# A hybrid decoder layer on one core: gates between heads, loads ahead, operands without a store, sums on VectorE

## The chip, the core and the metric

One core of one Trainium2 chip runs the whole program. Five engines work side by side, each through its own queue in order: TensorE (PE: matrix products, into PSUM), VectorE (DVE), ScalarE (ACT), GpSimd (POOL) and the sync engine (SP), which issues most DMAs; POOL and ACT issue some too. The metric is the time of one execution on the device, in microseconds, as the median of several. A difference of 0.3% is about what can be measured here.

## The reference, cut to what matters

One layer, for a prompt of 1024 tokens and for 8 sample sequences of 4 tokens each (32 columns more), all in float32:

```python
proj = x @ w_in                            # q,k,v | hgrn q,f,i,g | gate_a | gate_b
oa = rms_norm((softmax(q1 k1^T) - lam*softmax(q2 k2^T)) v) * (1 - lam_init)   # 4 heads; sample: paged cache, 1024 old tokens
ob = rms_norm(hgrn2_scan(...)) * silu(g)                                       # 4 heads
merged = sigmoid(ga) * (oa @ w_branch_a) + sigmoid(gg) * (ob @ w_branch_b)
h = layer_norm(ALPHA * x + merged @ w_out)
a, g = split(h @ w_up);  c = conv3(a) + b                                      # D_FF = 2816
out = layer_norm(ALPHA * h + (gelu(c) * g) @ w_down)
```

## The kernel before, in words

**Products.** Every operand of a large product is split into a rounded part and a remainder (`split`, L131: a cast on ScalarE, L132, a subtraction on VectorE, L133), and each product is three matmuls (L238 to L240). So whatever PE reads costs both engines some time first.

**Order.** The program is written in the order below. A planner lays each engine's queue out from it: it runs the program against its own estimate of durations and gives an engine the earliest instruction in program order that it holds ready. On the chip each queue is then fixed. A tile of a tag with n buffers waits until one of these is given back.

**Attention and gates.** The input projection is done in pieces. The sixteen gate blocks (`do_gates`, L845, through `proj_gate`, L830) are 72 matmuls each, a tanh and a store to DRAM (`gsc`). Two run before the first head, three after head 0, two after head 1, and nine after head 3, in the loop at L950. A head (`attn`, L615) goes through eight blocks of queries: scores, maximum, exponential, difference of the two softmaxes, transposes, product with v; its output goes to DRAM (`osc`).

**Sample.** `SampleAttn` works through the cached pages beside other work: sixteen steps (`beside`, L942), eight of keys and then eight of values. A step fetches two pages of 1 MB by indirect DMA from POOL's queue (L726) into two buffers; for keys VectorE transposes them (L746), PE multiplies (L752 for keys, L803 for values). The last value step of each group of four stores its output (`oss`). Before, ten steps stand in the gates' loop, four in the first half's merge (after every second block), two after its tiles 1 and 3.

**Merge, in two halves of the tokens.** `load_o` (L925) loads attention's output, eight tiles `Ot[k]` of 128 rows, splits it into the tags q0 to q7. `merge` (L1018) multiplies it by the branch weights in eight blocks m, with the gates in tags "ae" and "c", into `Mg`; then the output product, tile by tile of 128 tokens (`w_out`, two halves of columns), the LayerNorm statistics (L1106 to L1118), and `turn_` (L1055), which transposes the normalised rows on PE, scales and shifts the eight pieces (two of each four on VectorE, L1070, two on ScalarE, L1072) into "hs" tiles, and stores them to DRAM (`hT`, L1073, POOL's queue). `turn_` of a tile runs one tile late; that of the last tile is put into `pending`, which the next stage runs. The second `load_o` stands after the first merge.

**Operands of the up projection.** It is done as seven products instead of eight, of quarters of the operand (B11, B12, B21, B22) and of their sums (`combine`, L993: four sums, five pairs put; `put`, L983, splits). A quarter pair comes from token tile t of the first half and tile t + 4 of the second (`tile_operands`, L1008). Tiles 4 and 5 are summed straight from `turn_`; tiles 6 and 7 are loaded back from `hT` (`quad`, L987), tile 6's after the merge, tile 7's after the first chunk of the first up block. "hs" has three buffers, "ae" and "c" two.

**Up, conv, down.** Twenty-two up blocks m, each in two chunks of columns (256 and 272); the products are evacuated through two "hs" tiles (`Mt`, `Xt`, L1183), convolved in a row that lives in slots 2 and 3 of `rt` by turns (m even in 2, odd in 3), and stored (`uT`). `down_half` (L1240) loads the 22 tiles in pairs, through one buffer of its own and `rt` 2 and 3 in turn, splits them and multiplies.

Of the kernel before, what the change touches and what calls it, by code (L numbers as in the profile page):

```python
# [44 lines left out]
def hybrid_step(ctx: ExitStack, tc: tile.TileContext, I, O):  # L45
# [835 lines left out]
    do_gates(2)  # L881
    Q, K = proj_q(1, q_slots()), K1
    attn(2, Q[0], K[0], v[0])
    sample_new_scores()
    attn(3, Q[1], K[1], v[1])
    psx.close()
# [35 lines left out]

    wba, wbb, wout = I["w_branch_a"][0], I["w_branch_b"][0], I["w_out"][0]

    def load_o(th, nh):  # L925
        Ot = [qt(k) for k in range(8)]
        for k in range(8):
            raw = wide(("hs", "ae")[k % 2])
            if k < 4 or nh == 512:
                SY.dma_start(raw[:, :nh], osc[k][:, th:th + nh])  # L930
            else:
                SY.dma_start(raw[:, :512], osc[k][:, th:th + 512])
                SY.dma_start(raw[:, 512:nh], oss[k - 4])
            split(raw[:, :nh], Ot[k][:, 0, :nh], Ot[k][:, 1, :nh])
        return Ot

    av = avs.enter_context(tc.tile_pool(name="av", bufs=1))
    ap = aps.enter_context(rpool("ap"))
# [8 lines left out]
        if len(steps) == 8:  # L947
            aps.close()

    for n in (2, 1, 1, 1, 1, 1, 1, 1, 1):  # L950
        do_gates(1)
        if len(gates) == 2:
            Ot = load_o(*HALVES[0][:2])
        beside(n)
    px.close()

# [36 lines left out]
    def combine(c, cols, b11, b12, b21, b22, t3):  # L993

        G.tensor_tensor(t3, b22, b12, ALU.subtract)
        G.tensor_tensor(b12, b12, b11, ALU.subtract)
        put(c, B22, cols, b22)
        G.tensor_tensor(b22, b22, b12, ALU.subtract)
        put(c, T2, cols, b22)
        G.tensor_tensor(b21, b21, b22, ALU.subtract)  # L1000
        put(c, T1, cols, b12)
        put(c, T3, cols, t3)
        put(c, T4, cols, b21)
# [1 line left out]
    def tile_cols(t):  # L1005
        return t // 2, slice(t % 2 * 128, t % 2 * 128 + 128)

    def tile_operands(t, b12=None, b22=None):  # L1008

        c, cols = tile_cols(t)  # L1010
        if b12 is None:
            b12, b22 = quad("ae", 0, 1, t), quad("c", 1, 1, t)
        b11, b21 = quad("ae", 0, 0, t), quad("c", 1, 0, t)
        combine(c, cols, b11, b12, b21, b22, wide("hs")[:, :512].rearrange("p (k t) -> p k t", k=4))

# [2 lines left out]
    def merge(Ot, half, beside=None):  # L1018
# [5 lines left out]
        for m in range(8):  # L1024
# [18 lines left out]
            if beside and m % 2:  # L1043
                beside(1)


        tiles = (4, 5, 8, 6, 7) if half else tiles
        rr = []
# [5 lines left out]

        def turn_(r, t, tt, tn):  # L1055

            ys = f2.tile([128, 2, 4, TS], F32, tag="ys", name="ys") if t == 8 else None
            yy = []
            for h2 in range(2):
                p = (ps_s.tile([128, 512], F32, tag="s", name="ps_s") if h2 else pst()).rearrange("p (k t) -> p k t", k=4)  # L1060
                y = ys[:, h2] if t == 8 else wide("hs")[:, :512].rearrange("p (k t) -> p k t", k=4)
                yy.append(y)
                for k4 in range(4):
                    k = h2 * 4 + k4
                    transpose(p[:, k4, :tn], r[:tn, k * 128:(k + 1) * 128])
                for k4 in range(4):
                    k = h2 * 4 + k4
                    g1, b1 = pt[:, P_L1G + k:P_L1G + k + 1], pt[:, P_L1B + k:P_L1B + k + 1]
                    if k4 >= 2:
                        V.tensor_scalar(y[:, k4, :tn], p[:, k4, :tn], g1, b1, ALU.mult, ALU.add)  # L1070
                    else:
                        S.activation(y[:, k4, :tn], p[:, k4, :tn], AF.Identity, bias=b1, scale=g1)  # L1072
                G.dma_start(hT[h2][half][:, :, tt - th:tt - th + tn].rearrange("k p t -> p k t"), y[:, :, :tn])  # L1073
            if t == 8:
                ts_ = f2.tile([128, 4, 16], F32, tag="ts", name="ts")
                cols = slice(256, 272)
                b = [ys[:, i, :, j:j + 16] for i in range(2) for j in (0, 16)]
                put(1, B11, cols, b[0])
                put(1, B21, cols, b[2])
                combine(1, cols, *b, ts_)  # L1080
            elif t in (4, 5):
                tile_operands(t - 4, *yy)

        if half:
# [8 lines left out]
        for hf, some in ((0, tiles[:2]), (1, tiles), (0, tiles[2:])) if half else ((0, tiles), (1, tiles)):  # L1093
            w = w_B(wout, hf * 512, 512)
            for t, r in zip(tiles, rr):
                if t not in some:
                    continue
                tt, tn = tok(t)
                lt = tt - th
                ps = pmm()  # L1100
                rv = r[:tn, hf * 512:(hf + 1) * 512]
                if t < 8:
                    mm3(ps, [((Mg[k][:, 0, lt:lt + tn], Mg[k][:, 1, lt:lt + tn]), w[k]) for k in range(KD)])
                else:
                    mm_s(ps[:2 * TS], Ms, w)
                    V.scalar_tensor_tensor(rv, rv, 2.0 * ALPHA, ps[TS:2 * TS], ALU.mult, ALU.add)  # L1106
                V.scalar_tensor_tensor(rv, rv, 2.0 * ALPHA if t < 8 else 1.0, ps[:tn], ALU.mult, ALU.add)
                st = sts[:, t % 4 + (t == 8) * 4]
                V.bn_stats(st[:tn, hf], rv)
                if t not in done:  # L1110
                    done.add(t)
                    if beside and t % 2:
                        beside(1)
                    continue
                mu, rs = aggr(st, tn, 4.0 * EPS)
                nm = f2.tile([128, 1], F32, tag="nm", name="nm", bufs=2)[:tn]
                V.tensor_scalar(nm, mu, rs, -1.0, ALU.mult, ALU.mult)
                S.activation(r[:tn], r[:tn], AF.Identity, bias=nm, scale=rs)  # L1118
                for x in late:
                    turn_(*x)  # L1120
                late = [(r, t, tt, tn)]
        pending.extend((lambda x=x: turn_(*x)) for x in late)

    merge(Ot, 0, beside)
    avs.close()
    h0.append(ups.enter_context(tc.tile_pool(name="h0", bufs=1)))
    Ot = load_o(*HALVES[1][:2])
    merge(Ot, 1)
    tile_operands(2)


    w_up, w_dn = I["w_up"][0], I["w_down"][0]
# [39 lines left out]
    for m in range(NM):  # L1172
# [7 lines left out]
        S.copy(aes[:, :, 0:2], st_conv[:, m])  # L1180
        for c, cn in enumerate(CHUNK):
            x = ops[c]
            Mt, Xt = wide("hs"), wide("hs")  # L1183
            m1, m5, u3, u4 = Mt[:, :cn], Mt[:, 272:272 + cn], Xt[:, :cn], Xt[:, 272:272 + cn]
            o = c * 256

# [17 lines left out]
            if m + c == 0:  # L1204

                while pending:
                    pending.pop(0)()
                tile_operands(3)
        for hf, tag in enumerate(("ae", "c")):
            cc, o = wide(tag), hf * 512  # L1210
            S.activation(cc[:, :512], ae[:, o + 2:o + 514], AF.Identity, bias=cb, scale=cw[2])
# [28 lines left out]
    def down_half(half, before=None):  # L1240
# [2 lines left out]
        U = []  # L1243
        for k in range(NM):
            if k % 2 == 0:
                j = k // 2 % 3
                raw = rt(j + 1, (2, 544)) if j else us.tile([128, 2, 544], F32, tag="ur", name="ur")
            SY.dma_start(raw[:, k % 2, :nh], uT[k][:, th:th + nh])
            u = ut(k)
            split(raw[:, k % 2, :nh], u[:, 0, :nh], u[:, 1, :nh])  # L1250
            U.append(u)
# [189 lines left out]
```

## Time and profile before

| | |
|---|---|
| Median of 3 runs | 1845.83 us (1841.52 to 1846.64) |
| Profiled execution, its span | 1842.59 us, 1840.1 us |
| PE, PE's weight loads busy | 1730.7 us (94%), 1618.0 us (88%) |
| VectorE, ScalarE, POOL busy | 1103.8 us (60%), 765.5 us (42%), 579.4 us (31%) |
| Read from HBM, written | 172.44 MB, 40.41 MB |

The profile is one execution. Times of rows are microseconds from the span's start. In the slices, a digit is a share in tenths over a fortieth of the span. In a timeline, a row is one instruction or a run of equal ones; the last bracket is the engine's idle time before it and what ended that. PE's matmuls are pipelined, so a row's time is longer than the step from one to the next.

### The profile page before, as it was taken

How to read it: one execution, taken by the hardware profiler on the slowest of the kernel's cores; microseconds unless marked ns; L12 is line 12 of the kernel's file. 1: busy time of each engine (PE TensorE's matmuls, PEld its weight loads, DVE VectorE, ACT ScalarE, POOL GpSimd, SP SyncE). 2: the span in 40 equal slices, each digit the busy share in tenths (PEclk: the TensorE clock that was granted, in tenths of full speed). 3: DMA queues.
4: the chain of work that ended last, by engine and by line, in shares of the span. 5: the costliest groups of instructions: out<-in, count | busy, mean ns of one | idle time of the engine just before them, and what ended most of it. 6: DMA issues, size and time to landing. Idle time of an engine off the chain costs nothing.

```text
span 1840.1 us, 34341 instructions
## 1 busy us (share of the span) xinstructions
PE 1730.7 (94%) x13412; PEld 1618.0 (88%) x13412; DVE 1103.8 (60%) x2327; ACT 765.5 (42%) x1775; POOL 579.4 (31%) x735
## 2 busy tenths in 40 slices
PE   8999999999999798989979949999999997999995
PEld 8999999999999597967879749999999996888995
DVE  5767546654656655525466857767776776338435
ACT  6466253445553452213243534434444444325222
POOL 1000110430413122213121466776677663001003
PEclk9999999999999999989989869999999998999997
DMA  6110211221211028778576322322222227436443
GB/s 212 35 60 25 81 60 41 90 67 59 85 63 54 1 87 282 245 279 296 196 220 205 101 70 70 98 72 76 79 88 73 76 70 251 124 111 204 133 125 109
DMA packets 215273, 215.07 MB, mean 117 GB/s; under 512 B 11212, under 2 KB 182174, under 8 KB 211016
## 3 DMA queue, kind: packets, MB, share of 16 engines
q1 hardware_dynamic: 190944, 136.04, 24.5%
q0 software_dynamic: 17040, 67.99, 10.3%
q10 hardware_dynamic: 7128, 8.86, 1.4%
q8 instruction: 105, 1.72, 0.4%
q14 instruction: 56, 0.46, 0.1%
HBM read 172.44 MB, written 40.41 MB: 116 GB/s over the span
## 4 chain that ended last, share of the span: by engine, by line
PE 48%; DMA 7%; DVE 4%; issue 3%; ACT 2%; POOL 1%; SPq 0%; ACTq 0%; POOLq 0%; DVEq 0%
PE mm L1268 4%; PE mm L1267 4%; PE mm L1269 4%; PE mm L1168 4%; PE mm L1167 4%; PE mm L1166 4%; PE mm L238 3%; PE mm L239 3%; PE mm L240 3%; PE ps_s L1167 2%; PE ps_s L1168 2%; PE ps_s L1166 2%; PE tp L1167 2%; PE tp L1168 2%; PE tp L1166 2%
## 5 line engine op out<-in xcount | busy, mean ns | idle before, releaser
L133 DVE TENSOR_TENSOR wl<-raw,wh 128x512 fp32r<-128x512 f32 x378 | 271.6, 728 | 235.2 <-ACT wh L132 195.8
L132 ACT CAST wh<-raw 128x512 fp32r<-128x512 f32 x378 | 226.7, 609 | 405.5 <-PE mm L1268 116.7
L238 PE MATMUL mm<-xh,wh 128*128 128x384 f32 (+1 forms) x560 | 186.9, 334 | 0.4 <-ACT wh L132 0.3
L240 PE MATMUL mm<-xh,wl 128*128 128x384 f32 (+1 forms) x560 | 186.4, 333 | 0.0
L239 PE MATMUL mm<-xl,wh 128*128 128x384 f32 (+1 forms) x560 | 185.9, 332 | 0.0
L238 PE MATMUL mm<-wh,xh 128*128 128x256 f32 x480 | 136.0, 284 | 1.4 <-DVE rb L581 1.4
L239 PE MATMUL mm<-wl,xh 128*128 128x256 f32 x480 | 136.3, 285 | 0.2 <-DVE wl L133 0.2
L240 PE MATMUL mm<-wh,xl 128*128 128x256 f32 x480 | 135.7, 284 | 0.0
L1267 PE MATMUL mm<-q,wh 128*128 128x512 f32 (+2 forms) x384 | 124.8, 325 | 0.0
L1269 PE MATMUL mm<-q,wl 128*128 128x288 f32 (+2 forms) x384 | 124.7, 326 | 0.1
L1268 PE MATMUL mm<-q,wh 128*128 128x512 f32 (+2 forms) x384 | 124.4, 324 | 0.0
L240 PEld LDWEIGHTS mm<-xh,wl 128*128 128x128 f32 x560 | 105.4, 188 | 3.7 <-issue 3.6
L238 PEld LDWEIGHTS mm<-xh,wh 128*128 128x128 f32 x560 | 105.3, 188 | 2.6 <-issue 1.5
L239 PEld LDWEIGHTS mm<-xl,wh 128*128 128x128 f32 x560 | 105.5, 188 | 0.9 <-issue 0.6
L238 PEld LDWEIGHTS mm<-wh,xh 128*128 128x128 f32 x480 | 90.3, 188 | 2.0 <-issue 1.6
L239 PEld LDWEIGHTS mm<-wl,xh 128*128 128x128 f32 x480 | 90.2, 188 | 1.0 <-DVE wl L133 0.8
L240 PEld LDWEIGHTS mm<-wh,xl 128*128 128x128 f32 x480 | 90.3, 189 | 0.1
L1276 POOL DMA_DIRECT2D c<-hT x24 | 13.0, 540 | 221.9 <-PE mm L1269 76.2
L1167 PE MATMUL mm<-h,wh 128*128 128x256 f32 x264 | 75.8, 287 | 3.4 <-DVE h L133 3.4
L1166 PE MATMUL mm<-h,wh 128*128 128x256 f32 x264 | 75.6, 286 | 2.5 <-ACT wh L132 2.5
L1267 PEld LDWEIGHTS mm<-q,wh 128*128 128x128 f32 x384 | 72.5, 189 | 5.7
L1269 PEld LDWEIGHTS mm<-q,wl 128*128 128x128 f32 x384 | 72.4, 189 | 5.7 <-DVE wl L133 0.3
(504 smaller groups left out, 5492.1 us busy)
## 6 DMA issues: line engine op xcount, KB each, us to landing
raw<-in_w_in_dram SPq DMA_DIRECT2D x44, 512.0 KB
raw<-in_w_up_dram SPq DMA_DIRECT2D x44, 512.0 KB
raw<-in_w_down_dram SPq DMA_DIRECT2D x36, 512.0 KB
raw<-in_w_out_dram SPq DMA_DIRECT2D x20, 512.0 KB
raw<-in_w_down_dram SPq DMA_DIRECT2D x18, 384.0 KB
gsc<-gt ACTq DMA_DIRECT2D x32, 192.0 KB
uT<-ae POOLq DMA_DIRECT2D x22, 256.0 KB, 2.3
uT<-c POOLq DMA_DIRECT2D x22, 256.0 KB, 2.3
```

The source lines that it names most:

```text
L132: S.copy(h, src)
L133: eng.tensor_tensor(l, src, h.bitcast(F32), ALU.subtract)
L238: PE.matmul(ps, lhsT=ah, rhs=bh, start=(i == 0), stop=False)
L239: PE.matmul(ps, lhsT=ah, rhs=bl, start=False, stop=False)
L240: PE.matmul(ps, lhsT=al, rhs=bh, start=False, stop=(i == n - 1))
L1166: PE.matmul(ps, lhsT=ah, rhs=bh, start=(k == 0), stop=False)
L1167: PE.matmul(ps, lhsT=ah, rhs=bl, start=False, stop=False)
L1168: PE.matmul(ps, lhsT=al, rhs=bh, start=False, stop=(k == 3))
L1267: PE.matmul(ps, lhsT=ah, rhs=bh, start=(k == 0), stop=False)
L1268: PE.matmul(ps, lhsT=ah, rhs=bl, start=False, stop=False)
L1269: PE.matmul(ps, lhsT=al, rhs=bh, start=False, stop=(k == NM - 1))
L1276: G.dma_start(y, hT[m // 4][half][m % 4, :, c0:c0 + cn])
```

## The change

1. The two gates asked for between heads 2 and 3 are taken from the nine after head 3. The loop after the heads then runs seven gates with nine sample steps (2, 1, 1, 1, 1, 2, 1); the other seven steps stand in the first merge, four in its block loop and one after each tile.
2. `load_o(1)` stands inside the first merge, after its block loop and before its output tiles, loads 512 columns a tile, in "c" and "ae" buffers instead of "hs" and "ae". The 32 sample columns come after the first merge, by five DMAs from POOL's queue (`load_os`).
3. `turn_` gives all eight pieces to ScalarE. Tiles 6 and 7 go through `tile_operands` straight from `turn_`, as 4 and 5 do. The first chunk of the first up block is evacuated through "ae" and "c".
4. In `combine`, three of the four sums run on VectorE.
5. The down projection's pairs go through the buffers in the order 0, 2, 0, 2, 0, 3, 2, 0, 3, 2, 0 (0 is its own).

```diff
@@ the heads
     attn(2, Q[0], K[0], v[0])
+    do_gates(2)
     sample_new_scores()
     attn(3, Q[1], K[1], v[1])
@@ load_o
-    def load_o(th, nh):
+    def load_o(half):
         Ot = [qt(k) for k in range(8)]
         for k in range(8):
-            raw = wide(("hs", "ae")[k % 2])
-            if k < 4 or nh == 512:
-                SY.dma_start(raw[:, :nh], osc[k][:, th:th + nh])
-            else:
-                SY.dma_start(raw[:, :512], osc[k][:, th:th + 512])
-                SY.dma_start(raw[:, 512:nh], oss[k - 4])
-            split(raw[:, :nh], Ot[k][:, 0, :nh], Ot[k][:, 1, :nh])
+            raw = wide(("c", "ae")[k % 2])[:, :512]
+            SY.dma_start(raw, osc[k][:, half * 512:half * 512 + 512])
+            split(raw, Ot[k][:, 0, :512], Ot[k][:, 1, :512])
         return Ot
+    def load_os(Ot):
+        raw = f2.tile([128, 8, TS], F32, tag="ys", name="os8")
+        for k in range(4):
+            G.dma_start(raw[:, k], osc[k][:, TP:T])
+        G.dma_start(raw[:, 4:], oss.rearrange("h p t -> p h t"))
+        for k in range(8):
+            split(raw[:, k], Ot[k][:, 0, 512:], Ot[k][:, 1, 512:])
@@ the gates' loop
-    for n in (2, 1, 1, 1, 1, 1, 1, 1, 1):
+    for n in (2, 1, 1, 1, 1, 2, 1):
@@ combine
         G.tensor_tensor(t3, b22, b12, ALU.subtract)
-        G.tensor_tensor(b12, b12, b11, ALU.subtract)
+        V.tensor_tensor(b12, b12, b11, ALU.subtract)
         put(c, B22, cols, b22)
-        G.tensor_tensor(b22, b22, b12, ALU.subtract)
+        V.tensor_tensor(b22, b22, b12, ALU.subtract)
         put(c, T2, cols, b22)
-        G.tensor_tensor(b21, b21, b22, ALU.subtract)
+        V.tensor_tensor(b21, b21, b22, ALU.subtract)
@@ merge, after the loop over m
+        ahead = None if half else load_o(1)
@@ turn_
-                    if k4 >= 2:
-                        V.tensor_scalar(y[:, k4, :tn], p[:, k4, :tn], g1, b1, ALU.mult, ALU.add)
-                    else:
-                        S.activation(y[:, k4, :tn], p[:, k4, :tn], AF.Identity, bias=b1, scale=g1)
+                    S.activation(y[:, k4, :tn], p[:, k4, :tn], AF.Identity, bias=b1, scale=g1)
...
-            elif t in (4, 5):
+            elif half:
                 tile_operands(t - 4, *yy)
@@ merge, the first pass over a tile
-                    if beside and t % 2:
+                    if beside:
                         beside(1)
@@ between the merges and after
-    merge(Ot, 0, beside)
+    Ot = merge(Ot, 0, beside)
+    load_os(Ot)
     avs.close()
     h0.append(ups.enter_context(tc.tile_pool(name="h0", bufs=1)))
-    Ot = load_o(*HALVES[1][:2])
     merge(Ot, 1)
-    tile_operands(2)
@@ up blocks
-            Mt, Xt = wide("hs"), wide("hs")
+            Mt, Xt = (wide("hs"), wide("hs")) if m + c else (wide("ae"), wide("c"))
...
                 while pending:
                     pending.pop(0)()
-                tile_operands(3)
@@ down_half
             if k % 2 == 0:
-                j = k // 2 % 3
-                raw = rt(j + 1, (2, 544)) if j else us.tile([128, 2, 544], F32, tag="ur", name="ur")
+                j = (0, 2, 0, 2, 0, 3, 2, 0, 3, 2, 0)[k // 2]
+                raw = rt(j, (2, 544)) if j else us.tile([128, 2, 544], F32, tag="ur", name="ur")
```

## Rows read from the trace of the kernel before

**Rows 1.** The page's slices of 46 us: busy tenths, granted clock in tenths.

```profile
PE   8999999999999798989979949999999997999995
...
PEclk9999999999999999989989869999999998999997
```

**Rows 2.** Waits of PE, whole span: what waited, releaser, total us, times, longest.

```profile
PE ps_s L1166 <- ACT q L132: 14.6, 1, 14.6
PE mm L1267 <- ACT x L132: 12.8, 1, 12.8
...
PE tp L220 <- ACT r L1118: 9.1, 2, 6.9
```

**Rows 3.** Stretches: length, busy us of each engine, clock, DMA share, GB/s.

```profile
592.00:646.00 54.00, 38.61 (x218) 31.30 (x217) 37.52 (x123) 26.30 (x74) 7.53 (x21) 0.91 0.00 1
...
664.00:704.00 40.00, 39.63 (x256) 39.63 (x257) 17.34 (x37) 15.19 (x40) 10.89 (x17) 1.00 0.61 211
704.00:803.00 99.00, 93.32 (x1492) 79.81 (x1491) 47.60 (x58) 19.82 (x42) 23.60 (x39) 0.98 0.70 240
...
816.00:925.00 109.00, 107.26 (x794) 84.58 (x790) 55.54 (x104) 32.85 (x60) 28.53 (x27) 0.98 0.75 260
...
1044.00:1097.00 53.00, 26.70 (x137) 23.86 (x135) 32.12 (x58) 20.44 (x45) 30.96 (x32) 0.71 0.28 82
```

**Rows 4.** Timeline of POOL, 680 to 816: start, us, what, idle before and releaser.

```profile
689.03 1.05 POOL L726 DMA_INDIRECT pg<-in_cache_k_dram,idx  x1 [0.16 <-issue]
...
766.67 0.94 POOL L726 DMA_INDIRECT pg<-in_cache_k_dram,idx  x1 [8.07 <-DVE pw L746]
...
776.08 0.94 POOL L726 DMA_INDIRECT pg<-in_cache_k_dram,idx  x1 [5.92 <-DVE pw L746]
...
785.16 0.94 POOL L726 DMA_INDIRECT pg<-in_cache_v_dram,idx  x1 [5.45 <-DVE pw L746]
```

**Rows 5.** Timeline of PE, 798 to 824.

```profile
800.84 1.96 PE L803 MATMUL tp<-pg,aT 128*32 128x128 f32 x64
...
817.71 0.79 PE L238 MATMUL mm<-q,wh 128*128 128x512 f32 x1
```

**Rows 6.** Timeline of PE, 924 to 944.

```profile
924.59 0.40 PE L239 MATMUL mm<-wl,q 128*128 128x512 f32 x1
924.83 0.40 PE L240 MATMUL mm<-wh,q 128*128 128x512 f32 x1
...
939.34 0.82 PE L238 MATMUL mm<-q,wh 128*128 128x256 f32 x2 [1.96 <-ACT q L132]
...
943.57 0.29 PE L240 MATMUL mm<-q,wl 128*128 128x256 f32 x1
```

**Rows 7.** Timeline of ACT, 926 to 945.

```profile
938.64 0.64 ACT L132 CAST q<-hs 128x544 fp32r<-128x544 f32 x1 [3.29 <-DMA hs<-osc]
```

**Rows 8.** Timeline of POOL, 1054 to 1100.

```profile
1055.22 1.27 POOL L995 TENSOR_TENSOR hs<-hs 128x512 f32<-128x512 f32 x1 [1.19 <-DVE r L133]
...
1087.83 0.75 POOL L1073 DMA_DIRECT2D hT<-hs  x1
```

**Rows 9.** Timeline of ACT, 1044 to 1100.

```profile
1061.38 0.80 ACT L1072 ACTIVATE hs<-tp,pt 128x128 f32<-128x128 f32 x2 [3.79 <-DVE r L133]
...
1095.57 0.62 ACT L132 CAST q<-c 128x512 fp32r<-128x512 f32 x1 [7.85 <-DMA c<-hT]
```

**Rows 10.** Timeline of DVE, 1050 to 1098.

```profile
1051.45 0.63 DVE L133 TENSOR_TENSOR wl<-S,wh 128x512 fp32r<-128x512 f32 x1
...
1057.63 3.72 DVE L133 TENSOR_TENSOR r<-hs,h 128x512 fp32r<-128x512 f32 x1 [0.27 <-ACT h L132]
```

**Rows 11.** Timeline of PE, 1536 to 1560.

```profile
1539.97 0.40 PE L1269 MATMUL mm<-x,wl 128*128 128x512 f32 x1
1553.15 0.80 PE L1267 MATMUL mm<-x,wh 128*128 128x512 f32 x1 [12.78 <-ACT x L132]
```

**Rows 12.** Timeline of SP's queue, 1510 to 1570.

```profile
1547.09 1.15 SPq L1248 DMA_DIRECT2D r<-uT  x2
```

More of the change, by code (lines that the diff above doesn't have):

```diff
@@ L948, in beside @@
             aps.close()
-    for n in (2, 1, 1, 1, 1, 1, 1, 1, 1):
+    for n in (2, 1, 1, 1, 1, 2, 1):
         do_gates(1)
         if len(gates) == 2:
-            Ot = load_o(*HALVES[0][:2])
+            Ot = load_o(0)
         beside(n)
@@ L1006, in tile_cols, with tile_operands @@
         return t // 2, slice(t % 2 * 128, t % 2 * 128 + 128)
-    def tile_operands(t, b12=None, b22=None):
+    def tile_operands(t, b12, b22):
         c, cols = tile_cols(t)
-        if b12 is None:
-            b12, b22 = quad("ae", 0, 1, t), quad("c", 1, 1, t)
         b11, b21 = quad("ae", 0, 0, t), quad("c", 1, 0, t)
@@ L1055, in turn_ @@
         def turn_(r, t, tt, tn):
-            ys = f2.tile([128, 2, 4, TS], F32, tag="ys", name="ys") if t == 8 else None
+            ys = f2.tile([128, 8, TS], F32, tag="ys", name="ys").rearrange("p (a k) t -> p a k t", a=2) if t == 8 else None
             yy = []
@@ L1122, in merge @@
         pending.extend((lambda x=x: turn_(*x)) for x in late)
-    merge(Ot, 0, beside)
+        return ahead
+    Ot = merge(Ot, 0, beside)
+    load_os(Ot)
     avs.close()
     h0.append(ups.enter_context(tc.tile_pool(name="h0", bufs=1)))
-    Ot = load_o(*HALVES[1][:2])
     merge(Ot, 1)
-    tile_operands(2)
     w_up, w_dn = I["w_up"][0], I["w_down"][0]
```

## The prediction, made before the result was known

> **What bounds the kernel now.** I read the slices first. The reader is to see that TensorE (PE) is full in nearly all of them, that the gaps stand in slices 14 to 18, 21, 24, 34 and 40, and that the granted clock is lower in 18, 21, 23, 24, 34 and 40 [rows 1]. So the time is PE's work plus what PE loses in a handful of places, and a change is worth what it takes out of those. The waits of PE, by total, name three of them: 14.6 us in one piece for a cast into an operand of the up projection, 12.8 us in one piece for a cast of the down projection's input, 9.1 us in two pieces for rows normalised by the first LayerNorm [rows 2]. The table of stretches gives the rest [rows 3]: the last two heads (592 to 646) have PE busy 38.61 of 54.00 us, the sample's keys (704 to 803) 93.32 of 99.00, the first half's merge (816 to 925) 107.26 of 109.00, the start of the up projection (1044 to 1097) 26.70 of 53.00 at a mean clock of 0.71. The change touches each of these places. I take them in order of time, against the profiled execution's 1842.59 us (span 1840.1, 2.5 around it); the median of the runs shown is 1845.83, 3.2 above it.
>
> **Gates between heads 2 and 3, and the sample beside fewer gates.** A gate is 72 matmuls. Between 664 and 704 PE runs nearly nothing else: 256 matmuls in 39.63 us [rows 3], so a gate is about 72 x 0.155 = 11.1 us and two are 22.2. Between 592 and 646 PE idles 54.00 - 38.61 = 15.4 us. If the planner lays the two gates into all of that, attention ends 22.2 - 15.4 = 6.8 us later than now; if into none, 22.2. I take 13 us filled, so attention ends 9.2 later and seven gates follow instead of nine.
>
> What they covered there has its own pace. The pages of the sample's cache come in pairs into two buffers, and a page is fetched when its forerunner has been transposed: the first at 689.03, the last two pairs of keys at 766.67 and 776.08, the first values at 785.16 [rows 4]. That is 96.1 us for eight steps, 12.0 each, and 9.4 at the best. The first value step ran at 800.84 (64 records, 1.96 us), the merge's first matmul at 817.71 [rows 5]. If the chain of pages stays as it is, the merge can start at 802.8 + 9.2 = 812.0, 5.7 earlier, but 1.5 value steps, now done before it, come into it (1.5 x 1.96 = 3 us). Left: 2.7. With two gates fewer in PE's queue ahead of the key products I let the chain gain another 2.5. Sum -5. Bounds: +10 (nothing filled: 22.2 - 14.9 + 3.0) and -25 (nearly all idle time of 592 to 817 gone).
>
> Seven value steps now lie in the merge, the last three a single tile apart: 24 matmuls of 0.24 (924.59 to 924.83, [rows 6]) = 5.8 us, plus 2 for the step, against 9.4 for a pair of pages. Unless the planner spreads them, that is 3 x 1.6 = 5 us of waiting at most; I leave it in the range.
>
> The turned pieces that go from VectorE to ScalarE in the first half (four a tile, 0.40 each) lie under the same 109 us, of which ScalarE is busy 32.85 [rows 3], and cost nothing.
>
> **The second half's attention output split ahead.** PE ends the first half's last output tile at 925.2 and starts the second half's first product at 939.34; the first products then take 0.41 each where the same shape takes 0.29 from 943.57 on [rows 6]. What ended the wait is the cast of the first tile of attention output, itself waiting for its load into an "hs" buffer [rows 7]; LayerNorm's turned tiles use the same three buffers. In the new order all eight loads and splits stand ahead of the output tiles, in buffers that the merge's loop has finished with. Moved: eight loads of 256 KB on SP's queue, past the x rows and w_out, eight casts and eight subtractions, which lie under 816 to 925, where VectorE is busy 55.54 of 109 us and ScalarE less. The sample's columns come by five small loads on POOL's queue and sixteen small splits; the first block's first chunk doesn't need them, so I cost them at nothing; without that cover its second chunk would wait some 3 us. Gone: 939.34 - 925.2 = 14.1, less some 2 for 16 transposes that stay, and about half of the slow 4 us. Next late is tile 3's normalised row, but its transposes now have products beside them. I take -12; the ends are -16 and 0.
>
> **Operands straight from LayerNorm, sums on VectorE.** Now tile 7 of the last four is stored at 1087.83 on POOL's queue [rows 8], loaded again, cast at 1095.57 after 7.85 us of waiting [rows 9], and with the end of that cast, at 1096.2, PE's wait of 14.6 us ends [rows 2]. In the new code tiles 6 and 7 are summed where they stand, so store, load and two pairs of loads leave the path. Tile 5's first sum, at 1055.22, waits for a VectorE split that frees a buffer [rows 8]; the change doesn't touch that, so I start there. From then a tile needs on VectorE three sums and five subtractions of 128x512, 0.63 each where nothing disturbs them [rows 10], some 5.2 us, and on ScalarE eight turned pieces at 0.40 [rows 9], 3.2 us, as the four that VectorE did move there. Three tiles one behind the other: 1055.2 + 5.2 + 1.5 (the sample's small ones) + 2 x 8.4 = 1079, where now tile 7's first such operand lands at 1096.2 and four sums are still to come: over 17 us earlier. Also gone: the first chunk's results no longer wait for "hs". Against it stand the second block's weight splits (7 x 0.65) and the evacuations of two chunks (some 4 us), which now fall into the same stretch on VectorE. I take -17. Ends: +3 and -30 (all the idle time of 1044 to 1097, 26.3, and some of the slow clock).
>
> In this stretch one VectorE split took 3.72 us instead of 0.63 [rows 10], while POOL ran sums back to back. The Trainium skill (SBUF — State Buffer, "Who interferes with whom") says that a VectorE instruction with two SBUF inputs and a GpSimd instruction that reads SBUF exclude one another for the whole instruction. The trace agrees. By that rule the move cuts both ways: fewer POOL sums block VectorE, but each sum on VectorE can be blocked by the one that stays on POOL and by the weights' four, which is rival (b).
>
> **The down projection's loads.** PE did 12 matmuls to 1540.4 and then waited until 1553.15, 12.78 us [rows 11], for a pair in slot 3, whose load was issued at 1547.09 [rows 12], when the last conv row, which lives there, was done. In the new order slot 3 first holds the sixth pair. Ten tiles come ahead of it: 30 matmuls of 0.24 [rows 6] = 7.2 us in place of 12 x 0.24 = 2.9. The wait shrinks by 4.3; the load itself comes no earlier. -4; ends -9 and +2 (two buffers in turn instead of three).
>
> **Sum.** -5 - 12 - 17 - 4 = -38: 1842.6 - 38 = 1804.6. Runs lie up to 4 above the profiled one, so I add 1.4: **1806 us**.
>
> **The rivals.** (a) Pages pace the sample stage: the two gates are not missed where they were, and lengthen attention where they are. For it: fetches wait for transposes all along [rows 4]; against it: PE is full in much of the stage [rows 3]. The first term is +8: 1819.
> (b) VectorE becomes the bound at the start of the up projection: twelve sums, the splits and the evacuations queue up, and the third term is -6: 1817. As in the split of 3.72 us, each of the nine sums of tiles 5 to 7 could be held up by one POOL sum of 1.27 us [rows 8], 11 us, which makes -17 into -6. Against it: VectorE itself idles 53 - 32.12 = 20.9 us there [rows 3].
> (c) Slower: the chain of value pages ends the first half. Nothing is filled (+22.2), the pages start as much later, the three last steps wait out 5 us more each (+15), less 14.9 - 3.0 of slack; the sample's output then comes after the merge, and the split ahead gains nothing: with the third term between forecast and (b), at -13, that is +25 + 0 - 13 - 4 = +8, 1852 with the 1.4. It decides as soon as the last value step ends behind the last output tile. Against it: pairs of pages came 9.4 apart.
> (d) Better: the planner draws the merge's first blocks into the pages' waits, and the first term is -18: 1793.
> (e) The planner's new order doesn't carry out what the code says: no change, 1845.
>
> **How the numbers follow.** Forecast 0.45 (its own range 1795 to 1818), (a) 0.20, (b) 0.12, (d) 0.12, (c) 0.07, (e) 0.04. The range that leaves out two in ten goes from the better part of (d) to (a) and (b) together (+8 - 12 - 6 - 4 = -14, 1830) and a little over: 1787 to 1836. A difference under 0.3% (5.5 us) can't be told from none here; faster by more than that are the forecast, (a), (b) and (d) but for a tail of 0.02: 0.87 (0.45 + 0.20 + 0.12 + 0.12 - 0.02); within 0.3%: (e) and 0.01: 0.05; slower: (c) and 0.01: 0.08.
>
> **What would show it.** Right: gate matmuls among head 2's; the second half's first product within 3 us of the last output tile; no wait over 6 us between 1044 and 1097; some 8 us of wait at the down projection's start. Wrong: attention longer by over 15 us; PE waiting on value pages for over 15 us in the merge; VectorE busy without a gap while the first up block waits; a store between tile 7's LayerNorm and its sums still on the chain.

## The result, and the profile after

The changed kernel takes 1790.70 us (median of 4 runs, 1788.99 to 1793.11), the kernel before, beside it, 1844.84 us (4 runs, 1841.52 to 1846.64): a ratio of 0.9709, 95% interval 0.969 to 0.9729. The forecast was 1806 us, in a range of 1787 to 1836. Its sign and its stated range held; the range that it gave to its own sum, 1795 to 1818, did not. The forecast was 15 us too high, 11.5 of them in the sum (1804.6 against 1793.1 for the profiled execution), the rest in the allowance for the median, and the reasons of its four terms were in part others than it named.

The profiled execution took 1793.11 us, its span is 1791.3 us. The page's slices of the changed kernel, busy tenths and granted clock, are to be read against [rows 1]:

```profile
PE   8999999999999989889999979999999999999995
...
PEclk9999999999999999989999979999999999999997
```

The gaps of slices 21 (between the merges) and 34 (the start of down) are gone. That of the heads (7 tenths in slice 14) has shrunk to 8 tenths in slice 15; the sample's keys (8 tenths, now in 17 and 18) and the start of up (24, now 7 instead of 4 tenths) still show. The prediction counted slices 15 and 17 among the gaps before, which stand at 9 tenths there; nothing in it hangs on that. PE's waits in the changed kernel, by total (what waited, releaser, us, times, longest), against [rows 2]:

```profile
PE mm L238 <- ACT wh L132: 8.1, 2, 7.5
...
PE ps_s L1169 <- ACT q L132: 4.9, 1, 4.9
...
PE mm L238 <- DVE c L1039: 3.1, 1, 3.1
...
PE mm L1270 <- ACT wh L132: 2.5, 2, 2.2
```

The 14.6 us before tile 7's operands have become 4.9, and the 12.8 us at the down projection are gone: what is left there is for weights, not for the input: 2.5 us in the last row, and 1.3 more for their remainders. New are 7.5 us in one piece for a cast of branch weights and 3.1 us for VectorE's product with a gate. Three stretches of the changed kernel, each laid on the work of one in [rows 3] or behind it:

```profile
592.00:646.00 54.00, 51.42 (x334) 49.07 (x332) 36.68 (x107) 29.14 (x80) 6.83 (x18) 1.00 0.13 41
...
913.00:1024.00 111.00, 106.98 (x649) 94.43 (x649) 72.92 (x139) 55.49 (x123) 31.48 (x31) 0.98 0.64 199
1024.00:1077.00 53.00, 40.55 (x276) 38.69 (x275) 48.66 (x82) 33.45 (x77) 26.85 (x30) 0.81 0.26 78
```

In the heads, PE's idle time fell from 15.4 to 2.6 us of 54 and the mean granted clock rose from 0.91 to 1.00. At the start of the up projection, PE is busy 40.55 us of 53 instead of 26.70, at a clock of 0.81 instead of 0.71.

Where the time went is seen best in a few landmarks of PE's timeline, us from the span's start (the last column is what the stage gained or lost):

| | before | after | of the stage |
|---|---|---|---|
| attention's last store | 682.3 | 689.0 | +6.7 |
| first matmul of the merge | 817.7 | 786.1 | |
| last matmul of the first half's output product | 924.8 | 913.1 | -18.4 |
| second half's first product | 939.3 | 913.3 | -14.3 |
| first product of up | 1044.6 | 1024.5 | +5.9 |
| first product of down | 1537.4 | 1497.3 | -20.0 |
| last product of down | 1815.3 | 1766.6 | -8.6 |
| end | 1840.1 | 1791.3 | -0.1 |

Together -48.8 us of the profiled execution. The rows of PE behind the second to fourth line, in the changed kernel:

```profile
777.82 0.85 PE L752 MATMUL tp<-pw,q 32*32 32x256 f32 x12
786.14 0.80 PE L238 MATMUL mm<-q,wh 128*128 128x512 f32 x1 [7.46 <-ACT wh L132]
...
913.06 0.40 PE L240 MATMUL mm<-wh,q 128*128 128x512 f32 x1
913.30 0.28 PE L238 MATMUL mm<-q,wh 128*128 128x256 f32 x1
```

Before, the first merge matmul came after the first value step [rows 5]. Now it stands among the keys, whose last matmul (L752) runs at 808.0, and the two halves follow each other without the gap of [rows 6].

### The profile page after: what moved, and what is told of

The parts are those of the page before. It is cut to its first block, busy times and chain, and to the rows that moved or that the text cites. A ratio compares the mean times of both kernels' runs of the same rounds, so it can differ in the third digit from the quotient of the medians.

```text
span 1791.3 us, 34307 instructions
## 1 busy us (share of the span) xinstructions
PE 1721.9 (96%) x13412; PEld 1612.1 (90%) x13412; DVE 1096.7 (61%) x2314; ACT 776.6 (43%) x1819; POOL 561.5 (31%) x725
## 4 chain that ended last, share of the span: by engine, by line
PE 48%; DMA 8%; DVE 3%; ACT 2%; issue 2%; POOL 1%; ACTq 0%; SPq 0%; DVEq 0%; POOLq 0%
PE mm L1169 4%; PE mm L1170 4%; PE mm L1171 4%; PE mm L1270 4%; PE mm L1272 4%; PE mm L1271 4%; PE mm L238 3%; PE mm L239 3%; PE mm L240 3%; DMA pg<-in_cache_k_dram,idx 2%; PE ps_s L1170 2%; PE ps_s L1171 2%; PE ps_s L1169 2%; PE tp L1170 2%; PE tp L1171 2%; PE tp L1169 2%
## 5 line engine op out<-in xcount | busy, mean ns | idle before, releaser
L1272 PE MATMUL mm<-q,wl 128*128 128x512 f32 (+2 forms) x384 | 124.9, 326 | 0.1
L216 ACT COPY s<-tp 128x512 f32<-128x512 f32 (+3 forms) x96 | 39.8, 424 | 87.3 <-PE tp L665 31.5
L1270 PEld LDWEIGHTS mm<-q,wh 128*128 128x128 f32 x384 | 72.5, 189 | 5.7
L1271 PEld LDWEIGHTS mm<-q,wh 128*128 128x128 f32 x384 | 72.5, 189 | 5.7
```

The costliest lines, as they stand in the source:

```text
L216: S.copy(out, in_)
L1270: PE.matmul(ps, lhsT=ah, rhs=bh, start=(k == 0), stop=False)
L1271: PE.matmul(ps, lhsT=ah, rhs=bl, start=False, stop=False)
L1272: PE.matmul(ps, lhsT=al, rhs=bh, start=False, stop=(k == NM - 1))
```

## The experiments

Each kernel was timed in five rounds beside the kernel before. Behind each median stand, in brackets, its ratio to that kernel and the 95% interval of the ratio; the signed number is the difference from the changed kernel's median (1790.7). Such a difference is good to some 3 us: the median of the kernel before itself lay between 1841.2 and 1844.8 us beside the different groups of runs.

**Gates back behind head 3.**

```diff
     attn(2, Q[0], K[0], v[0])
-    do_gates(2)
...
-    for n in (2, 1, 1, 1, 1, 2, 1):
+    for n in (2, 1, 1, 1, 1, 1, 1, 1, 1):
...
-                    if beside:
+                    if beside and t % 2:
```

> The changed kernel with its first part alone undone: nine gates after head 3 again, nine sample steps beside them and one more, six in the first merge. Theory A (the planner fills the waits of the keys with the first blocks of the merge as soon as gates run out earlier): the whole first term as the two traces put it comes back, +11.7 us, 1802.4 us, and the first merge matmul stands behind the first value step, some 32 us later than in the changed kernel. Theory B (only the idle time of the last two heads was won, as forecast): +5, 1796. Rival C (the chain of pages sets the end of the stage in both): 0, 1791.

1803.24 us (0.9791, 0.9771 to 0.981): +12.5, theory A. The stretch of the heads, and PE at the merge's start, in this kernel:

```profile
592.00:646.00 54.00, 37.85 (x223) 31.24 (x221) 37.78 (x123) 26.84 (x76) 9.07 (x22) 0.92 0.02 5
```

```profile
815.51 1.93 PE L803 MATMUL tp<-pg,aT 128*32 128x128 f32 x32 [3.90 <-DMA pg<-in_cache_v_dram,idx]
817.37 0.80 PE L238 MATMUL mm<-q,wh 128*128 128x512 f32 x1
```

Both are the kernel before again: idle time and low clock in the heads, and a merge that starts only after value steps that wait for pages. So the two gates do two things: they fill the heads, and, being gone from behind them, they let the planner draw the merge's blocks between the keys. This run undoes both at once and does not say how much each is worth.

**One gate instead of two between the heads.**

```diff
-    do_gates(2)
+    do_gates(1)
...
-    for n in (2, 1, 1, 1, 1, 2, 1):
+    for n in (2, 1, 1, 1, 1, 1, 1, 1):
```

> The changed kernel with one gate between heads 2 and 3 instead of two, eight after head 3, the sample steps as in the changed kernel. The merge's first blocks still stand among the keys' last two steps. Theory A (PE's own work bounds from head 2 on): some 4 to 5 us of idle time stay in the heads, +4, 1795. Rival B (the pages pace the stage, and start when attention ends): attention ends some 5 us earlier, the last value step too, and the sample's output is less late for the second merge: -4, 1787.

1800.07 us (0.9751, 0.9724 to 0.9777): +9.4, twice what theory A said; B falls, for attention ended no earlier (690.7 against 689.0). From 560 to 910, the first line of this kernel, the second of the changed one:

```profile
560.00:910.00 350.00, 321.36 (x3158) 278.61 (x3156) 191.58 (x434) 116.19 (x292) 88.19 (x139) 0.95 0.55 190
```

```profile
560.00:910.00 350.00, 327.32 (x3171) 283.55 (x3173) 194.88 (x440) 119.39 (x296) 88.24 (x140) 0.96 0.56 190
```

PE idles 28.6 us instead of 22.7 there, and not at all from 910 to the end of its output product. That end comes 9.8 us later. Of these, 2.1 were there before the heads (a gate's store at 561.9 against 559.7), 5.9 are the idle time, and the rest I have not taken apart. In the heads (592 to 646) PE idles 6.3 us instead of 2.6, which is theory A's part; the rest of the idle time lies among the pages, where PE's waits for transposed keys are 13.4 us instead of 5.3, while the wait of 7.5 us for branch weights is gone.

**The second half's attention output, place and buffers.** Three kernels make a square with the changed one. First the place alone:

```diff
-        ahead = None if half else load_o(1)
+        ahead = None
...
-    Ot = merge(Ot, 0, beside)
-    load_os(Ot)
+    merge(Ot, 0, beside)
...
-    merge(Ot, 1)
+    Ot = load_o(1)
+    load_os(Ot)
+    merge(Ot, 1)
```

> The changed kernel with the second half's attention output loaded and split after the first merge again, in its new buffers and with the sample's columns apart. Forecast: +12 us, 1803. From the landmarks: the gap of 14.3 us between the halves comes back; if the 5.9 us that the second merge is longer are the price of having the products start early (they only run into the next late thing), they vanish and the sum is +8.4, 1799; if they are the price of the separate loads of the sample's columns, they stay and it is +14.3, 1805. Rival: the gap was one of the three hs buffers alone, which these loads no longer use: below +6, 1797.

1791.10 us (0.9722, 0.9702 to 0.9742): +0.4, as the rival said and no other theory. The loads on SP's queue tell why, in this kernel (first fence) and in the changed one (second):

```profile
844.19 0.32 SPq L931 DMA_DIRECT2D c<-osc  x1
...
859.73 0.32 SPq L931 DMA_DIRECT2D ae<-osc  x1
```

```profile
844.64 0.32 SPq L931 DMA_DIRECT2D c<-osc  x1
...
860.57 1.15 SPq L931 DMA_DIRECT2D ae<-osc  x1
```

In these buffers the planner draws them to the same spot from either place. So the same kernel with the old buffers:

```diff
-            raw = wide(("c", "ae")[k % 2])[:, :512]
+            raw = wide(("hs", "ae")[k % 2])[:, :512]
```

> As the kernel with the second half's attention output split after the first merge, and its loads in hs and ae buffers again, as before; the sample's columns still apart. That kernel took 1791.1 us, no more than the changed kernel, and its loads stood at the same place in the queue. Theory: not the place in the program but the tag did it, since hs tiles come in turn behind LayerNorm's, c and ae tiles don't; then the gap between the halves is back, 10 to 14 us long, less the 4 us of waits for the sample's columns that it covers: +6 to +14, 1797 to 1805. Rival: the gap was closed by the earlier end of the merge, whatever the buffers: 0, 1791.

1806.73 us (0.979, 0.9763 to 0.9818): +16.0. The four hs loads (SP), the cast (ACT) and PE's waits in this kernel:

```profile
929.54 5.62 SPq L931 DMA_DIRECT2D hs<-osc  x4
```

```profile
933.00 0.62 ACT L132 CAST q<-hs 128x512 fp32r<-128x512 f32 x1 [3.52 <-DMA hs<-osc]
```

```profile
926.28 1.11 PE L220 MATMUL ps_s<-ident,r 128*128 128x128 f32 x4 [4.18 <-ACT hs L1075]
933.67 0.82 PE L238 MATMUL mm<-q,wh 128*128 128x256 f32 x2 [6.27 <-ACT q L132]
```

That is the gap of [rows 6, 7], 21 us long (912.5 to 933.7). And the old buffers at the new place:

> The changed kernel with the loads of the second half's attention output at their new place in the program, but in hs and ae buffers as before. It completes a square: new place and c buffers 1790.7 us, old place and c buffers 1791.1, old place and hs buffers 1806.7. Theory (a load can be drawn ahead of whatever comes after it in the turn of its buffers; at the new place the hs tiles come ahead of LayerNorm's): place alone is enough as well, within 3 us of 1791. Rival (hs tiles are late wherever they stand, because LayerNorm's turned rows hold them): +10 or more, 1801 or more.

1796.16 us (0.9753, 0.9729 to 0.9778): +5.5, between the two. Its gap is closed (the products meet at 913.6), so the place is enough against the gap: with the old buffers it is worth 10.6 us, with the new ones 0.4. What this kernel lost lies in the second merge (115.2 us from the first product to up's, 111.2 in the changed kernel), where PE's waits are 7.0 us instead of 4.0; why they are longer is open.

**The sample's late output.** The second merge had grown by 5.9 us. To try whether the sample is why, four heads' sample columns were read from another tensor:

```diff
-        G.dma_start(raw[:, 4:], oss.rearrange("h p t -> p h t"))
+        for k in range(4, 8):
+            G.dma_start(raw[:, k], osc[k][:, 512:512 + TS])
```

> The changed kernel, but the 32 sample columns of the four attention heads are read from the head of the prompt's attention output, not from the sample's, which is thereby left out of the result. If the late sample output (last value step at 910, store at 920, load at 924, split at 927) is what makes the second merge longer, the three waits of 0.5, 0.4 and 3.1 us go: -4, 1787. Rival: those waits come from the gates' buffers, which are given back late for other reasons: 0, 1791.

1784.25 us (0.9672, 0.9645 to 0.9699): -6.5. Its second merge takes 105 us, without an idle one:

```profile
911.00:1016.00 105.00, 105.00 (x652) 93.26 (x651) 73.74 (x136) 55.21 (x120) 31.51 (x30) 1.00 0.65 209
```

So the sample's output is what makes it longer. The chain in the changed kernel, on POOL, ACT and VectorE: the second chunk waits for the sample's columns, then gives back its gate buffers late, and a later gate is loaded late (last row; PE's 3.1 us wait for that instruction):

```profile
920.26 0.84 POOL L827 DMA_DIRECT2D oss<-soc  x1 [2.29 <-DVE soc L826]
...
924.14 0.75 POOL L940 DMA_DIRECT2D os<-oss  x1 [1.67 <-DMA oss<-soc]
```

```profile
927.16 0.58 ACT L132 CAST q<-os 128x32 fp32r<-128x32 f32 x4 [0.47 <-DMA os<-oss]
```

```profile
929.28 0.42 DVE L1040 SCALAR_TENSOR_TENSOR ae<-ae,mm 128x256 f32<-128x256 f32 x1 [1.32 <-PE mm L240]
...
938.56 0.78 DVE L1039 SCALAR_TENSOR_TENSOR c<-c,mm 128x256 f32<-128x256 f32 x2 [1.82 <-DMA c<-gsc]
```

The store and the load back can be had out of this chain, with the result whole:

```diff
-            oc = av.tile([128, 4, 16], F32, tag="soc", name="soc")
-            V.tensor_scalar(oc, p..., SUBG, None, ALU.mult)
-            G.dma_start(oss[:, :, g * 16:g * 16 + 16]..., oc)
+            V.tensor_scalar(os8[:, 4:, g * 16:g * 16 + 16], p..., SUBG, None, ALU.mult)
...
+    os8 = f2.tile([128, 8, TS], F32, tag="ys", name="os8")
+    for k in range(4):
+        G.dma_start(os8[:, k], osc[k][:, TP:T])
     sample = SampleAttn(ap, av)
```

> The changed kernel, with the sample's output written by VectorE straight into the tile that the second merge splits, in place of a store to DRAM and a load back; the other four heads' columns are loaded before the sample's steps. Theory: with the store at 920 and the load at 924 gone, the split can run some 7 us earlier, at 920, before the first block needs it, and the 6.4 us by which the run without the sample's output was shorter come off: -4 to -7, 1784 to 1787. Rival: the last value step itself is the late one, and the planner puts what it gains elsewhere: within 2 us of 1791.

1790.93 us (0.9722, 0.97 to 0.9743): +0.2, nothing won, the rival. In its second merge PE still waits 3.2 us, against 4.0 in the changed kernel. The four loads that this edit puts ahead of the sample's steps stand ahead of the pages on POOL's queue (in the changed kernel the planner has them behind the first pair, at 697.9), and the last value step (PE) now runs behind the last output product, whose last matmul starts at 908.6:

```profile
694.49 2.14 POOL L942 DMA_DIRECT2D os<-osc  x4 [3.93 <-ACT gt L831]
...
699.06 1.29 POOL L726 DMA_INDIRECT pg<-in_cache_k_dram,idx  x1 [0.18 <-issue]
```

```profile
909.49 2.18 PE L803 MATMUL tp<-pg,aT 128*32 128x128 f32 x64
```

The first page came 3.6 us later than in the changed kernel (695.5), 1.0 of it because attention ended later; PE's first key matmul came 7.3 later (717.3 against 710.0). The chain was shortened at its end and lengthened at its start. Whether it is worth its 6 us with the four loads behind the pages was not tried, so that the loads' place is the reason is not shown. That kernel with a third gate between the heads:

```diff
-    do_gates(2)
+    do_gates(3)
...
-    for n in (2, 1, 1, 1, 1, 2, 1):
+    for n in (2, 1, 1, 2, 2, 1):
```

> The kernel before this one in the list (sample's output kept on the chip), with three gates between heads 2 and 3 instead of two; the merge's first blocks then stand among five steps of the keys. Theory A (the idle time of the heads is used up by two gates; a third lengthens attention by its 11 us and is made good in the stage behind, but no more): within 3 us of that kernel. Rival B (pages pace the stage, and attention ends later): +5 or more against it. Rival C (more of the merge beside the keys is better): -3 or less against it.

1804.54 us (0.9794, 0.977 to 0.9818): +13.6 against the two gates, theory B. The heads and the second merge, and the last value step (PE), in this kernel:

```profile
908.00:1035.00 127.00, 115.09 (x780) 100.67 (x779) 73.61 (x143) 55.12 (x123) 31.89 (x31) 0.95 0.64 207
560.00:650.00 90.00, 90.00 (x642) 88.42 (x640) 60.70 (x177) 42.10 (x123) 17.32 (x44) 1.00 0.20 64
```

```profile
926.09 1.93 PE L803 MATMUL tp<-pg,aT 128*32 128x128 f32 x32 [2.97 <-DMA pg<-in_cache_v_dram,idx]
```

PE has no idle time left in the heads, and the first half's products end as early as ever (907.9), but attention ends 9 us later (699.1 against 690.0), the pages with it, and the second merge takes 127 us.

**Tiles 6 and 7 through DRAM again.**

```diff
-            elif half:
+            elif t in (4, 5):
                 tile_operands(t - 4, *yy)
...
     merge(Ot, 1)
+    tile_operands(2)
...
                     pending.pop(0)()
+                tile_operands(3)
```

> The changed kernel with token tiles 6 and 7 loaded back from DRAM for the up projection's operands, as before; sums stay on VectorE, pieces on ScalarE, the first chunk in ae and c. If the store and the load back were the path: +17 (forecast) to +20 us (landmarks), 1808 to 1811, with one wait of over 10 us before tile 7's operands. Rival, the place of the sums was most of it: +6 or less, 1797 or less.

1800.43 us (0.9781, 0.9758 to 0.9804): +9.7, half of what was expected, and over the rival's 6. Its longest wait in up, by PE's waits, and the cast that ends it, which waits for a load back from `hT`:

```profile
PE ps_s L1172 <- ACT q L132: 10.0, 1, 10.0
```

```profile
1063.36 0.62 ACT L132 CAST q<-c 128x512 fp32r<-128x512 f32 x1 [6.91 <-DMA c<-hT]
```

**The sums back on GpSimd.**

```diff
-        V.tensor_tensor(b12, b12, b11, ALU.subtract)
+        G.tensor_tensor(b12, b12, b11, ALU.subtract)
```

and so the two other sums.

> The changed kernel with combine's three sums on GpSimd again. Theory A: on the path of tiles 5 to 7 nine sums of 1.27 us take the place of nine of 0.63: +6 us, 1797. Rival B (VectorE's sums and splits are held up beside GpSimd's, so that nothing was won by the move): within 2 us of 1791.

1803.15 us (0.9773, 0.9746 to 0.98): +12.4, twice theory A; rival B falls. POOL's timeline through the sums of tile 5 in this kernel:

```profile
1034.25 1.27 POOL L1002 TENSOR_TENSOR hs<-hs 128x512 f32<-128x512 f32 x1 [0.66 <-DVE r L133]
1035.46 0.78 POOL L1076 DMA_DIRECT2D hT<-ys  x1
1036.38 1.27 POOL L1152 TENSOR_TENSOR S<-raw 128x512 f32<-128x512 f32 x1
1037.61 1.26 POOL L1003 TENSOR_TENSOR hs<-hs,ae 128x512 f32<-128x512 f32 x1
...
1041.15 1.27 POOL L1005 TENSOR_TENSOR hs<-hs 128x512 f32<-128x512 f32 x1
...
1044.64 1.26 POOL L1007 TENSOR_TENSOR c<-c,hs 128x512 f32<-128x512 f32 x1
```

The sums (L1002 to L1007) stand some 3.5 us apart, since POOL runs without a gap: between two of them lie a store's issue, a sum of the second block's weights and smaller sums. Meanwhile a VectorE split that takes 0.68 us undisturbed takes 4.03 (this kernel):

```profile
1042.43 4.03 DVE L133 TENSOR_TENSOR h<-hs,h 128x512 fp32r<-128x512 f32 x1
```

VectorE's sums of the same tile in the changed kernel:

```profile
1032.91 0.68 DVE L1003 TENSOR_TENSOR hs<-hs,ae 128x512 f32<-128x512 f32 x1
...
1035.43 2.71 DVE L1005 TENSOR_TENSOR hs<-hs 128x512 f32<-128x512 f32 x1
...
1039.40 0.67 DVE L1007 TENSOR_TENSOR c<-c,hs 128x512 f32<-128x512 f32 x1
```

They stand 2.5 and 4.0 us apart, no closer, and one of them is held up as well; from the tile's first sum to the end of its last it is 9.0 us against 11.7. The larger difference is at tile 6, 9.2 us against 15.0: on VectorE its three sums stand 2.0 and 1.5 us apart, on POOL 3.2, and there they stand behind the up blocks' own work (a memset, then L1202 and L1205), before which POOL waits 4.25 us for VectorE (this kernel, POOL):

```profile
1054.89 0.10 POOL L1182 MEMSET r<- 128x2 f32 x1 [4.25 <-DVE ae L1201]
...
1056.38 1.33 POOL L1003 TENSOR_TENSOR hs<-hs,ae 128x512 f32<-128x512 f32 x1
```

So what the move took out is more than the 0.6 us of each sum: a place behind other work in POOL's queue, and the VectorE work that POOL's sums held up. How the 12.4 us divide between the two is not shown. PE's long wait in this kernel is 8.8 us, and it ends at 1066.8 instead of 1056.0.

**Two of four turned pieces on VectorE again.**

```diff
-                    S.activation(y[:, k4, :tn], p[:, k4, :tn], AF.Identity, bias=b1, scale=g1)
+                    if k4 >= 2:
+                        V.tensor_scalar(y[:, k4, :tn], p[:, k4, :tn], g1, b1, ALU.mult, ALU.add)
+                    else:
+                        S.activation(y[:, k4, :tn], p[:, k4, :tn], AF.Identity, bias=b1, scale=g1)
```

> The changed kernel with two of each four turned pieces on VectorE again. VectorE is busy 48.7 of the 53 us at the start of the up projection in the changed kernel. Theory A, VectorE is the tighter engine there: three tiles, four pieces each, some 0.3 us a piece: +3 to +4 us, 1794. Rival B, the pieces run beside other waits: within 2 us of 1791; rival C, ScalarE's eight pieces in a row are the longer chain and the old split is better: -2 or less.

1790.98 us (0.9727, 0.9705 to 0.975): +0.3, rival B. This part of the change is worth nothing that can be measured, though VectorE is busy 48.66 of the 53 us at the start of up in the changed kernel.

**Three buffers in turn for the down projection.**

```diff
-                j = (0, 2, 0, 2, 0, 3, 2, 0, 3, 2, 0)[k // 2]
-                raw = rt(j, (2, 544)) ...
+                j = k // 2 % 3
+                raw = rt(j + 1, (2, 544)) ...
```

> The changed kernel with the down projection's pairs in three buffers in turn again. Landmarks: +8.4 us, 1799, with a single wait of some 12 us at the start of the down projection. Forecast: +4, 1795. Rival, the buffers are indifferent and the gain came from what precedes: 0, 1791.

1800.65 us (0.9774, 0.9755 to 0.9793): +10.0, as the landmarks said. The wait is back in this kernel; in the changed one PE's longest in that place is 2.17 us:

```profile
1513.95 0.79 PE L1270 MATMUL mm<-x,wh 128*128 128x512 f32 x1 [11.13 <-ACT x L132]
```

```profile
1504.73 0.50 PE L1270 MATMUL mm<-x,wh 128*128 128x512 f32 x1 [0.37 <-ACT wh L132]
...
1510.86 0.50 PE L1270 MATMUL mm<-x,wh 128*128 128x512 f32 x1 [2.17 <-ACT wh L132]
```

Undone one by one, the parts cost 12.5 (gates), 16.0 (buffers and place of the attention output), 9.7 (tiles), 12.4 (sums), 0.3 (pieces) and 10.0 us (down): 60.9, where all of them together are 54.1. They overlap a little, if at all: six differences good to some 3 us each leave that open. No kernel with its result whole was faster than the changed one.

## Why the prediction was right, and where it was wrong

**Gates and sample, -5; it is -11.7 by the landmarks, 12.5 undone.** Attention ends 6.7 us later, near the 9.2 taken: of the 15.4 us of idle time 12.8 were filled, as good as the 13 forecast. From 560 to attention's last store PE idles 11.3 us less (5.5 against 16.8) and is busy 18.0 us longer, for work that the prediction priced at 22.2. That fits the granted clock, which it left out (at a mean of 0.91 over 54 us, 4.9 us of full-speed time had been missing, an estimate from [rows 3]; now it is 1.00); no run separates it. The step that failed is "If the chain of pages stays as it is, the merge can start at 802.8 + 9.2 = 812.0". The chain became longer (first value step 131.2 us after attention's last store, 118.5 before), but the merge did not wait for it: its blocks went in among the last keys, from 786.1 on. That is the mechanism of rival (d), which had been given 0.12 and -18. With nine gates left, the last gate product runs at 804.1, behind the last of the eight key steps (789.4); with seven it runs at 774.4, when two key steps are still to come (796.0 and 805.6), and the next in program order is the merge.

**Split ahead, -12; the gap shrank by 14.3, and 5.9 came back.** The mechanism was read rightly (the cast "itself waiting for its load into an "hs" buffer"). The change moves the loads and changes their buffers, and the square shows that either alone closes the gap: with the new buffers the place is worth 0.4 us more. The mis-sized term is the sample's columns, costed "at nothing; without that cover its second chunk would wait some 3 us". The cover was gone, since the merge ends 11.7 us earlier while the last value step comes 9.8 us later: the three waits are 4.0 us together, and the run without the sample's output was 6.5 us faster.

**Operands and sums, -17; it is -20.0.** The size is near, the division is not. The store and loads were to carry it; they carry 9.7 us, and the sums, which the prediction weighed as cutting both ways, carry 12.4: on POOL they stood behind other work and held VectorE up beside them. Rival (b) falls: VectorE did become the busiest engine of that stretch (48.66 of 53 us), and single splits are still held up for 2 us, but the part was worth more than forecast, not less. The pieces on ScalarE were costed at nothing in the first half, and put into the second half's chain at 3.2 us a tile; undone in both halves they are worth 0.3 us.

**Down loads, -4; it is -8.6 by the landmarks, 10.0 undone.** The 30 matmuls of ten tiles came as forecast (1497.27 to 1504.36), but not the 8 us of waiting behind them, and that is the term's error: while the pair in slot 3 was on its way, the planner laid the second output block's products on tiles already split into PE's queue, and these waited only for weights, 3.8 us in four pieces. With three buffers in turn only the first block's 12 matmuls of four tiles stand ahead of the wait, and 11.1 us of it remain.

**The signs and the rivals.** Gates among head 2's matmuls, the second half's first product within 3 us of the last output tile (0.2), no wait over 6 us at the start of up (longest 4.85): as named. The 8 us at the down projection's start: not. Rival (a), that the pages pace the stage, was wrong for two gates and right for three. Rival (c), slower through value pages behind the last output tile, did not come, but its mechanism is real: with three gates the last value step ran 18 us behind the first half's end, the second merge took 14.5 us longer than in the same kernel with two (126.9 against 112.4), and the whole 13.6. In the changed kernel the step runs 3 us before that end. It does not decide "as soon as" the step falls behind: in the kernel that kept the sample's output on the chip it started 0.5 us behind, at no loss that can be measured.

That the measured time lies in the stated range owes something to luck. The prediction's own mechanism gave 1795 to 1818; the range reached down to 1787 because of rival (d), which had 0.12, and it was (d)'s mechanism that came, while the first two terms erred in opposite directions (-11.7 for -5, -8.4 for -12).

## What to carry to other kernels

Where a planner lays out the queues, what holds a load back is whose turn its buffer is, so look for the tag that puts an early load behind a late user. A statement's place counts as far as it changes that turn: here 10.6 us in the shared buffers, 0.4 in others. Work moved out of a stage that waits for DMA can pay twice, once where it fills idle time and once because the next stage's work can be drawn into the gap it leaves, until the DMA chain's own end becomes the late thing. What a small operation costs on a shared engine is read from what stands ahead of it in that engine's queue and from what it holds up next door, not from its length.

## What the runs showed of the hardware

A load of 256 KB of branch weights, issued at 775.19 on SP's queue while pages of 1 MB were under way (from 770 to 786 the DMA engines were busy 83% of the time and moved 285 GB/s), was first read at 785.47 (ACT, changed kernel), and became PE's longest wait, 7.46 us:

```profile
785.47 0.62 ACT L132 CAST wh<-raw 128x512 fp32r<-128x512 f32 x1 [10.32 <-DMA raw<-in_w_branch_b_dram]
```

A VectorE subtraction with two SBUF inputs, 0.68 us undisturbed, took 2.36 us over a POOL sum, and ended 0.55 us after it (1055.46 + 2.36 = 1057.82; 1055.99 + 1.28 = 1057.27). The sum of 2.71 us above did the same (it ended at 1038.14, POOL's sum at 1037.59). VectorE's row and POOL's, changed kernel:

```profile
1055.46 2.36 DVE L133 TENSOR_TENSOR q<-c,q 128x512 fp32r<-128x512 f32 x1 [1.14 <-ACT q L132]
```

```profile
1055.99 1.28 POOL L1002 TENSOR_TENSOR hs<-hs 128x512 f32<-128x512 f32 x1
```

The Trainium skill (SBUF — State Buffer, "Who interferes with whom") says that such a pair exclude one another; the rows agree. So do the 4.03 us for one split with the sums back on POOL, where POOL runs without a gap: it ended 0.56 us after the last sum beside it (1046.46 against 1045.90). In each case VectorE's row starts before that POOL sum's, and it is VectorE that waits; why, the rows don't say. The prediction let the rule cut both ways; in this kernel the move was worth 12.4 us.
